# Moving the last gate quarter behind the last expert, and summing the outputs on VectorE

## The chip, the core and the metric

The kernel runs on one core of a Trainium2 chip. The metric is the time of one execution on the device in microseconds (us). A core has engines with a queue each: TensorE (PE in the profile: matrix products and transposes), VectorE (DVE), ScalarE (ACT), GpSimd (POOL) and the queue that issues most transfers (SP). An engine works through its queue in order and waits where an operand isn't ready. Matmul results go to PSUM (tiles pA, pB, pT, pG), all else lies in SBUF.

## The reference

A trunk of two layers over 512 tokens of width 1024. Layer 0 mixes with a state-space model and mean pools, layer 1 with stick-breaking attention. Each layer ends in a mixture of experts:

```
x = LN(alpha * x + mixer(x))
x = LN(alpha * x + MoE(x) + sigmoid(x Wg) * (p[i] Wp))

# attention, 16 heads of 64, strictly causal, by blocks of 128 queries
z = q k^T / 8
log_after = reverse cumsum of log_sigmoid(-z) over the causal keys, without the key itself
wts = exp(log_sigmoid(z) + log_after);  out = wts v

# LN: (x - mean) * rsqrt(var + 1e-5) * g + b
# MoE: 16 experts, router picks one group of four, in it the top two:
#   y_e = (silu(x W1) * (x W3)) W2,  MoE(x) = sum of gate * y_e over the token's two experts
```

All is float32; x is 512 x 1024, an expert's weights are 3 x 1024 x 512, Wg is 1024 x 1024 and Wp 256 x 1024.

## The kernel before

All matmuls that need float32 precision are done as three products of rounded parts: `split` (lines 84, 85) makes the high part with a ScalarE copy and the low part with a VectorE subtraction, `mm3` (89 to 91) issues the three. Weights come in pieces of 1 MB through a ring of 17 slots (tiles raw), each piece is split into w_0h, w_0l, w_2h, w_2l and so on. A scheduler orders the instructions of each engine by its own costs; the order is fixed when the program is built.

The tokens lie in four blocks of 128 rows: tiles x0r, listed `xt[0]` to `xt[3]`. `ffn` handles the experts in turn: each takes up to 96 tokens, gathered by index from a copy of x in memory (xd) with a transfer that POOL issues (line 936), turned, multiplied up (three 1024 x 512 pairs in all), through silu, multiplied down, and scattered to a table yd (line 942), two rows a token. Expert 12 is followed by a branch for tokens beyond the 96 (`overflow`). The last expert's output isn't scattered: it stays in SBUF as yl.

The gate sigmoid(x Wg) * (p Wp) is computed in four quarters of 256 columns (`gate`, lines 956 to 973). A quarter is 96 matmuls for x Wg (tile pG) and 24 for p Wp (tile pB), 128x256 each, in two halves of two blocks; then a sigmoid (966), a product (970) and, for each block, x = alpha * x + product (973). The tuple GATES sets where: quarter 0 ahead of the experts, quarters 1 to 3 behind experts 3, 6 and 10.

The tail (lines 1052 to 1076): the four tiles yt bring the two expert outputs of each token back, the last expert's product runs, and for each block and each half of 512 columns TensorE sums in PSUM: two matmuls with diagonal matrices of the token's gate values (dg) times yt (1068), and two with a one-hot matrix times yl (1071). VectorE adds x (1072) and takes statistics (1073); `ln_finish` (778 to 789) normalizes: bn_aggr and an addition (781, 782), the power -1/2 on POOL (783), and two steps over 1024 columns. The second is one VectorE step (789), or, with spread (blocks 0 to 2 of the tail), a ScalarE scaling (786) and a POOL addition (787). In layer 1 the block then goes out. In layer 0 it is turned (170) for the attention.

The attention (`attend`, 663 to 693) works on two heads at once, s = 0 and 1, and for each on four query blocks: scores (673 to 675), two sigmoids (678, 679), a scan (681), a product (682), then the weights are turned (686), copied (687) and multiplied with v (691). The two heads' products go to the lower and the upper half of one PSUM tile's partitions. Each is complete for one head before the other's, in the program's text.

The mixers' output projection (`out_proj`) adds x in `finish` (724), takes statistics (725) and calls `ln_finish` too.

## Time and profile before

| | us |
|---|---|
| median of three runs | 1267.3 (1264.76 to 1269.89) |
| the profiled execution | 1269.24 |
| its span in the trace | 1267.6 |
| TensorE busy | 1187.4 (94%) |
| VectorE busy | 972.6 (77%) |
| ScalarE busy | 748.4 (59%) |
| GpSimd busy | 152.2 (12%) |

The granted clock of TensorE over the span is 0.978. The stages as the trace has them: layer 0's mixer to about 210, its experts to 552, their tail to 587, the attention to 860, projection, normalization and router to 893, experts to 1236.6, tail to the end. Busy time is an average over these; a stage's limit is read from that stage.

### The profile page before, as it was taken

How to read it: one execution, taken by the hardware profiler on the slowest of the kernel's cores; microseconds unless marked ns; L12 is line 12 of the kernel's file. 1: busy time of each engine (PE TensorE's matmuls, PEld its weight loads, DVE VectorE, ACT ScalarE, POOL GpSimd, SP SyncE). 2: the span in 40 equal slices, each digit the busy share in tenths (PEclk: the TensorE clock that was granted, in tenths of full speed). 3: DMA queues.
4: the chain of work that ended last, by engine and by line, in shares of the span. 5: the costliest groups of instructions: out<-in, count | busy, mean ns of one | idle time of the engine just before them, and what ended most of it. 6: DMA issues, size and time to landing. Idle time of an engine off the chain costs nothing. (4 is left out here: it accounts for less than half of the span.)

```text
span 1267.6 us, 17418 instructions
## 1 busy us (share of the span) xinstructions
PE 1187.4 (94%) x6511; PEld 906.7 (72%) x6511; DVE 972.6 (77%) x1364; ACT 748.4 (59%) x1043; POOL 152.2 (12%) x160
## 2 busy tenths in 40 slices
PE   6958988999999999997999999998999999999895
PEld 5847778778787786756867877787677778787662
DVE  7996887896969967765477377868797887969676
ACT  4313523886868867842465455612687777868761
POOL 5010041010101000112000000012111000010004
PEclk9988999999999999998999999999999999999898
DMA  8235652998989998771113023543699797999842
GB/s 246 59 80 196 240 213 72 341 371 288 360 283 355 368 339 311 266 276 34 34 34 100 1 67 111 170 153 125 208 355 372 275 367 263 373 340 356 310 181 105
DMA packets 158165, 285.12 MB, mean 225 GB/s; under 512 B 19585, under 2 KB 43665, under 8 KB 157009
## 3 DMA queue, kind: packets, MB, share of 16 engines
q1 hardware_dynamic: 143760, 256.56, 58.0%
q0 software_dynamic: 9568, 25.19, 5.8%
q10 hardware_dynamic: 4736, 2.10, 0.6%
q8 instruction: 55, 0.90, 0.3%
q14 instruction: 46, 0.37, 0.1%
HBM read 272.02 MB, written 20.19 MB: 231 GB/s over the span
## 5 line engine op out<-in xcount | busy, mean ns | idle before, releaser
L85 DVE TENSOR_TENSOR w_0l<-raw,w_0h 128x1024 fp32r<-128x1024 f32 (+1 forms) x231 | 277.5, 1202 | 68.6 <-ACT w_0h L84 59.1
L84 ACT ACTIVATE w_0h<-raw 128x1024 fp32r<-128x1024 f32 (+1 forms) x233 | 242.8, 1042 | 76.8 <-PE pG L91 37.8
L85 DVE TENSOR_TENSOR w_2l<-raw,w_2h 128x1024 fp32r<-128x1024 f32 x205 | 249.7, 1218 | 21.9 <-ACT w_2h L84 21.7
L84 ACT ACTIVATE w_2h<-raw 128x1024 fp32r<-128x1024 f32 x205 | 216.6, 1056 | 44.6 <-PE pA L91 33.6
L89 PE MATMUL pA<-w_0h,g 128*96 128x512 f32 x256 | 105.6, 412 | 0.5 <-ACT g L84 0.5
L90 PE MATMUL pA<-w_0l,g 128*96 128x512 f32 x256 | 101.9, 398 | 0.0
L91 PE MATMUL pA<-w_2h,g 128*96 128x512 f32 x256 | 101.7, 397 | 0.0
L91 PE MATMUL pA<-w_0h,g 128*96 128x512 f32 x256 | 101.6, 397 | 0.0
L90 PE MATMUL pA<-w_2l,g 128*96 128x512 f32 x256 | 101.2, 395 | 0.0
L89 PE MATMUL pA<-w_2h,g 128*96 128x512 f32 x256 | 101.2, 395 | 0.0
L942 POOL DMA_INDIRECT yd<-ysb,ixm x30 | 32.1, 1071 | 489.5 <-ACT ysb L1038 489.5
L91 PEld LDWEIGHTS pA<-w_2h,g 128*96 128x96 f32 x256 | 41.6, 163 | 18.0
L91 PEld LDWEIGHTS pA<-w_0h,g 128*96 128x96 f32 x256 | 41.6, 163 | 17.9
L90 PEld LDWEIGHTS pA<-w_2l,g 128*96 128x96 f32 x256 | 41.6, 163 | 17.9
L89 PEld LDWEIGHTS pA<-w_2h,g 128*96 128x96 f32 x256 | 41.4, 162 | 17.8
L90 PEld LDWEIGHTS pA<-w_0l,g 128*96 128x96 f32 x256 | 42.2, 165 | 15.5 <-DVE w_0l L85 1.1
L89 PEld LDWEIGHTS pA<-w_0h,g 128*96 128x96 f32 x256 | 42.1, 164 | 14.9 <-ACT g L84 0.9
L936 POOL DMA_INDIRECT xg<-xd,ixm x32 | 35.3, 1104 | 138.1 <-PE pT L985 95.7
L89 PE MATMUL pB<-w_0h,sT 128*96 128x512 f32 x128 | 50.6, 396 | 1.2 <-ACT sT L84 1.2
L91 PE MATMUL pB<-w_0h,sT 128*96 128x512 f32 x128 | 51.2, 400 | 0.0
L90 PE MATMUL pB<-w_0l,sT 128*96 128x512 f32 x128 | 50.7, 396 | 0.4 <-DVE w_0l L85 0.4
L89 PE MATMUL pB<-w_2h,sT 128*96 128x512 f32 x128 | 51.0, 398 | 0.0
(439 smaller groups left out, 2874.2 us busy)
## 6 DMA issues: line engine op xcount, KB each, us to landing
raw<-in_moe_w_dram SPq DMA_DIRECT2D x192, 1024.0 KB, 11.4
raw<-in_sb_w_qkv_dram SPq DMA_DIRECT2D x12, 1024.0 KB, 7.9
raw<-in_ple_w_gate_dram SPq DMA_DIRECT2D x8, 1024.0 KB, 10.5
yt<-yd SPq DMA_DIRECT2D x8, 1024.0 KB, 8.0
raw<-in_ab_w_out_dram SPq DMA_DIRECT2D x4, 1024.0 KB, 6.4
xd<-x0r POOLq DMA_DIRECT2D x8, 512.0 KB, 2.9
raw<-in_sb_w_out_dram SPq DMA_DIRECT2D x4, 1024.0 KB, 6.0
raw<-in_ab_w_in_dram SPq DMA_DIRECT2D x3, 1024.0 KB, 9.7
```

The source lines that it names most:

```text
L84: return (self.nc.scalar.activation(hi, src, AF.Copy), (self.nc.gpsimd if pool else self.nc.vector).tensor_tensor(lo, src, hi.bitcast(F32) ...
L85: (self.nc.gpsimd if pool else self.nc.vector).tensor_tensor(lo, src, hi.bitcast(F32), op=OP.subtract))
L89: t.matmul(out, s[0], m[0], start=first, stop=False)
L90: t.matmul(out, s[0], m[1], start=False, stop=False)
L91: t.matmul(out, s[1], m[0], start=False, stop=last)
L936: return nc.gpsimd.indirect_dma_start(out=xgs[:CAP, e % 2, :], out_offset=None, in_=xd[:, :], in_offset=bass.IndirectOffsetOnAxis(ap=self. ...
L942: nc.gpsimd.indirect_dma_start(out=yd[:, :], out_offset=bass.IndirectOffsetOnAxis(ap=self.iy[:CAP, e:e + 1], axis=0), in_=src[:CAP], in_of ...
```

## The change

It has four parts. First, quarter 3 of the gate moves behind the last expert's down projection, and quarters 1 and 2 to experts 4 and 9; the scaling of x by alpha, for quarter 3's columns, becomes four steps of its own (line 1047 of the new file). Second, the tail's sum: instead of diagonal matrices on TensorE, VectorE adds each of the eight gate-weighted yt halves to x (line 1069, 128x1024 each); TensorE keeps the one-hot products. Third, statistics: bn_stats and bn_aggr go; the additions also give row sums (accum_out), ScalarE squares the centred block with a row sum, and no block is spread to POOL any more. Fourth, in the attention the two heads' products with v alternate, key block by key block, behind both heads' turns.

```diff
-GATES = (-1, 3, 6, 10)
+GATES = (-1, 4, 9, 15)
-SPF = (0, 1, 2)
-SPM = ()
# attend
+                kw = [self.half4("kw"), self.half4("kw")]
                 for s in range(2):
...
                     v.tensor_tensor(sg[:, :n - 1], sg[:, :n - 1], kp[:, 1:n], op=OP.mult)
+                for s in range(2):
+                    kp, sg = kw[s][:, :512], kw[s][:, 512:]
                     pT = self.bank("T", "pT")
                     for kb in range(qb + 1):
...
                     nc.any.tensor_copy(kp[:, :n], pT[:, :n])
-                    rows = slice(s * 64, s * 64 + 64)
-                    hc = (pg * 4 + h) * 64
-                    for kb in range(qb + 1):
-                        nc.tensor.matmul(po[rows, qs], vs[:, kb, hc:hc + 64], kp[:, kb * 128:(kb + 1) * 128],
-                                         start=(kb == 0), stop=(kb == qb))
+                for kb in range(qb + 1):
+                    for s in range(2):
+                        hc = (pg * 4 + 2 * o + s) * 64
+                        nc.tensor.matmul(po[s * 64:s * 64 + 64, qs], vs[:, kb, hc:hc + 64],
+                                         kw[s][:, kb * 128:(kb + 1) * 128], start=(kb == 0), stop=(kb == qb))
# out_proj, finish
-            v.scalar_tensor_tensor(xt[i][:, h], xt[i][:, h], ALPHA, ps, op0=OP.mult, op1=OP.add)
-            v.bn_stats(st[:, i, nh * 6:(nh + 1) * 6], xt[i][:, h])
+            v.scalar_tensor_tensor(xt[i][:, h], xt[i][:, h], ALPHA, ps, op0=OP.mult, op1=OP.add,
+                                   accum_out=st[:, i, nh:nh + 1])
# ln_finish
-        v.bn_aggr(mv[:, 0:2], st)
-        v.tensor_scalar(mv[:, 2:3], mv[:, 1:2], EPS, None, op0=OP.add)
+        v.tensor_scalar(mv[:, 0:1], st[:, 0:1], st[:, 1:2], -1.0 / D, op0=OP.add, op1=OP.mult)
+        sq = self.half4("sq")
+        nc.scalar.activation(sq, x, AF.Square, bias=mv[:, 0:1], accum_out=mv[:, 1:2])
+        v.tensor_scalar(mv[:, 2:3], mv[:, 1:2], 1.0 / D, EPS, op0=OP.mult, op1=OP.add)
         nc.gpsimd.tensor_tensor(mv[:, 3:4], mv[:, 2:3], self.mhalf, op=OP.pow)
-        v.scalar_tensor_tensor(x, x, mv[:, 0:1], self.lng, op0=OP.subtract, op1=OP.mult)
-        if spread:
-            nc.scalar.activation(x, x, AF.Copy, scale=mv[:, 3:4])
-            nc.gpsimd.tensor_tensor(x, x, self.lnb, op=OP.add)
-        else:
-            v.scalar_tensor_tensor(x, x, mv[:, 3:4], self.lnb, op0=OP.mult, op1=OP.add)
+        v.scalar_tensor_tensor(x, x, mv[:, 0:1], self.lng, op0=OP.add, op1=OP.mult)
+        v.scalar_tensor_tensor(x, x, mv[:, 3:4], self.lnb, op0=OP.mult, op1=OP.add)
# gate(c)
-                    v.scalar_tensor_tensor(x, x, ALPHA, sg[:, i], op0=OP.mult, op1=OP.add)
+                    if c < 3:
+                        v.scalar_tensor_tensor(x, x, ALPHA, sg[:, i], op0=OP.mult, op1=OP.add)
+                    else:
+                        v.tensor_tensor(x, x, sg[:, i], op=OP.add)
# behind expert 13
+                for i in range(NT):
+                    v.tensor_scalar(xt[i][:, 768:], xt[i][:, 768:], ALPHA, None, op0=OP.mult)
# tail
+        gate(3)
+        for i in range(NT):
+            for k in range(2):
+                v.scalar_tensor_tensor(xt[i], yts[i][:, k * D:(k + 1) * D], self.gates[:, k, i], xt[i],
+                                       op0=OP.mult, op1=OP.add)
         for i in range(NT):
             for nh in range(2):
...
-                for k in range(2):
-                    nc.tensor.matmul(p, dg[:, k * NT + i], yts[i][:, k * D + nh * 512:k * D + (nh + 1) * 512],
-                                     start=(k == 0), stop=False)
                 for a in range(2):
...
-                v.tensor_tensor(xt[i][:, h], p, xt[i][:, h], op=OP.add)
-                v.bn_stats(st[:, i, nh * 6:(nh + 1) * 6], xt[i][:, h])
-            self.ln_finish(xt[i], st[:, i], f"{layer}f{i}", i in SPF)
+                v.scalar_tensor_tensor(xt[i][:, h], p, 1.0, xt[i][:, h], op0=OP.mult, op1=OP.add,
+                                       accum_out=st[:, i, nh:nh + 1])
+            self.ln_finish(xt[i], st[:, i], f"{layer}f{i}")
```

The order of an engine's instructions is the scheduler's, so it is shown at three places. First TensorE in the first pair of heads of the attention. Before, around the products with v (691), the turns (686), scores (673 to 675) and the projection (89 to 91):

```order
L89 MATMUL pA<-x2Th_5581,w_4h 128x512
L691 MATMUL pA<-kw,v_5656 64x128
L686 MATMUL pT<-ident,kw 128x128 x2
L691 MATMUL pA<-kw,v_5656 64x128 x2
L686 MATMUL pT<-ident,kw 128x128 x3
L673 MATMUL pB<-KH,QS 128x512
L691 MATMUL pA<-kw,v_5656 64x128 x2
L674 MATMUL pB<-KL,QS 128x512
L675 LDWEIGHTS identb
```

After (the same lines are 691, 686 and 672 to 674, the projection 87 to 89):

```order
L691 MATMUL pA<-kw,v_5640 64x128 x4
L686 MATMUL pT<-ident,kw 128x128 x3
L89 MATMUL pA<-x2Th_5564,w_0l 128x512
L686 MATMUL pT<-ident,kw 128x128 x4
L87 MATMUL pA<-x2Th_5565,w_4h 128x512
L691 MATMUL pA<-kw,v_5640 64x128 x6
L686 MATMUL pT<-ident,kw 128x128 x4
L88 MATMUL pA<-x2Tl_5567,w_4h 128x512
L89 MATMUL pA<-x2Th_5565,w_4l 128x512
```

A group of products held one head's key blocks; now a group of four or more holds those of both heads in turn, behind the turns of both.

The second place is VectorE at the tail of layer 1. Before, from the last expert's output on (x0r_1245 holds blocks 0 and 1, x0r_1248 blocks 2 and 3):

```order
L1060 SCALAR_TENSOR_TENSOR yl_11783<-pB,gs,yl_11783 96x512 x2
L1072 TENSOR_TENSOR x0r_1245<-pA,x0r_1245 128x512
L1073 BN_STATS st1f<-x0r_1245 128x6
L1072 TENSOR_TENSOR x0r_1245<-pA,x0r_1245 128x512
L1073 BN_STATS st1f<-x0r_1245 128x6
L781 BN_AGGR mv1f_11856<-st1f 128x2
L782 TENSOR_SCALAR mv1f_11856<-mv1f_11856 128x1
L784 SCALAR_TENSOR_TENSOR x0r_1245<-x0r_1245,mv1f_11856,ln_ffn_11562 128x1024
L1072 TENSOR_TENSOR x0r_1245<-pA,x0r_1245 128x512
```

After, from the same instruction on (968 is the gate's product, 974 its addition, 1069 the sums of the expert outputs, 1077 the addition of the one-hot product):

```order
L1063 SCALAR_TENSOR_TENSOR yl_11614<-pB,gs,yl_11614 96x512 x2
L968 TENSOR_TENSOR sg<-sg,pB 128x512
L974 TENSOR_TENSOR x0r_1245<-x0r_1245,sg 128x256 x2
L1069 SCALAR_TENSOR_TENSOR x0r_1245<-yt_0_11606,gates_8027,x0r_1245 128x1024
L1069 SCALAR_TENSOR_TENSOR x0r_1245<-yt_1_11608,gates_8027,x0r_1245 128x1024
L1069 SCALAR_TENSOR_TENSOR x0r_1245<-yt_0_11606,gates_8027,x0r_1245 128x1024
L1069 SCALAR_TENSOR_TENSOR x0r_1245<-yt_1_11608,gates_8027,x0r_1245 128x1024
L968 TENSOR_TENSOR sg<-sg,pB 128x512
L1077 SCALAR_TENSOR_TENSOR x0r_1245,st1f<-pA,x0r_1245 128x512
L974 TENSOR_TENSOR x0r_1248<-x0r_1248,sg 128x256 x2
L1069 SCALAR_TENSOR_TENSOR x0r_1248<-yt_2_11610,gates_8027,x0r_1248 128x1024
```

The sums of blocks 0 and 1 stand ahead of the second half of the gate, those of blocks 2 and 3 behind it, and the normalization, which followed each block, comes behind all eight.

The third place is VectorE at layer 1's router, before the change (85 splits the turned x, 803 takes the logits):

```order
L85 TENSOR_TENSOR ol_5909<-pT,oh_5908 128x4x128
L85 TENSOR_TENSOR ol_6858<-pT,oh_6857 128x4x128
L85 TENSOR_TENSOR ol_5909<-pT,oh_5908 128x4x128
L85 TENSOR_TENSOR ol_6858<-pT,oh_6857 128x4x128
L803 COPY rt<-pB 32x512
L825 TENSOR_TENSOR rt<-rt,rbias 128x64
L828 TENSOR_TENSOR rt<-rt 128x32
```

After:

```order
L83 TENSOR_TENSOR ol_5893<-pT,oh_5892 128x4x128
L83 TENSOR_TENSOR ol_6842<-pT,oh_6841 128x4x128
L1047 TENSOR_SCALAR x0r_1245<-x0r_1245 128x256 x2
L1047 TENSOR_SCALAR x0r_1248<-x0r_1248 128x256 x2
L801 COPY rt<-pB 32x512
L823 TENSOR_TENSOR rt<-rt,rbias 128x64
L826 TENSOR_TENSOR rt<-rt 128x32
```

The four scalings of quarter 3's columns (1047) stand right ahead of the logits' copy (now 801). They write x, which the copies to xd read.

## Rows read from the trace of the kernel before

**Rows 1.** By stretch: us, busy PE, PEld, DVE, ACT, POOL; clock, DMA share, GB/s.

```profile
587.00:860.00 273.00, 269.57 (x1434) 207.98 (x1434) 171.30 (x277) 127.91 (x267) 10.88 (x9) 1.00 0.24 80
...
893.00:1236.60 343.60, 334.42 (x1738) 249.57 (x1738) 275.39 (x292) 261.25 (x318) 34.23 (x33) 0.99 0.89 314
1236.60:1267.60 31.00, 17.50 (x49) 8.77 (x47) 21.27 (x30) 4.13 (x4) 12.98 (x7) 0.82 0.24 98
```

**Rows 2.** POOL's timeline: start, length, line, tiles, the idle time before.

```profile
1109.40 1.09 POOL L942 DMA_INDIRECT yd<-ysb,ixm  x1 [15.30 <-ACT ysb L1038]
1127.07 0.94 POOL L942 DMA_INDIRECT yd<-ysb,ixm  x1 [14.90 <-ACT ysb L1038]
```

**Rows 3.** The table by stretch, an expert without a gate and one with it.

```profile
1032.00:1049.70 17.70, 17.70 (x118) 15.11 (x117) 11.32 (x13) 10.82 (x14) 0.94 (x1) 1.00 1.03 376
1127.07:1159.16 32.09, 32.09 (x207) 26.89 (x206) 21.90 (x26) 21.73 (x27) 1.90 (x2) 1.00 0.97 344
```

**Rows 4.** TensorE's timeline at the start of layer 1's tail.

```profile
1236.47 1.88 PE L1068 MATMUL pA<-yt,dg 128*128 128x512 f32 x4
```

**Rows 5.** VectorE's timeline in quarter 3 of layer 1's gate.

```profile
1133.46 0.69 DVE L970 TENSOR_TENSOR sg<-sg,pB 128x512 f32<-128x512 f32 x1 [4.46 <-PE pB L91]
...
1134.72 0.75 DVE L973 SCALAR_TENSOR_TENSOR x0r<-x0r,sg 128x256 f32<-128x256 f32 x2
```

**Rows 6.** VectorE's timeline in layer 1's tail.

```profile
1242.74 0.15 DVE L782 TENSOR_SCALAR mv1f<-mv1f 128x1 f32<-128x1 f32 x1
1242.81 1.27 DVE L784 SCALAR_TENSOR_TENSOR x0r<-x0r,mv1f,ln_ffn 128x1024 f32<-128x1024 f32 x1
1244.01 0.68 DVE L1072 TENSOR_TENSOR x0r<-pA,x0r 128x512 f32<-128x512 f32 x1
...
1247.17 2.05 DVE L784 SCALAR_TENSOR_TENSOR x0r<-x0r,mv1f,ln_ffn 128x1024 f32<-128x1024 f32 x1
...
1259.85 1.28 DVE L789 SCALAR_TENSOR_TENSOR x0r<-x0r,mv1f,ln_ffn 128x1024 f32<-128x1024 f32 x1 [0.44 <-POOL mv1f L783]
```

**Rows 7.** ScalarE's and POOL's timelines in layer 1's tail.

```profile
1244.55 1.15 ACT L786 ACTIVATE x0r<-x0r,mv1f 128x1024 f32<-128x1024 f32 x1 [7.19 <-POOL mv1f L783]
...
1245.78 2.35 POOL L787 TENSOR_TENSOR x0r<-x0r,ln_ffn 128x1024 f32<-128x1024 f32 x1 [1.27 <-ACT x0r L786]
...
1258.29 1.53 POOL L783 TENSOR_TENSOR mv1f<-mv1f,mhalf 128x1 f32<-128x1 f32 x1
```

**Rows 8.** TensorE's and VectorE's timelines in layer 0's tail.

```profile
552.28 7.03 PE L1068 MATMUL pA<-yt,dg 128*128 128x512 f32 x16
...
581.37 1.27 DVE L789 SCALAR_TENSOR_TENSOR x0r<-x0r,mv0f,ln_ffn 128x1024 f32<-128x1024 f32 x1
...
590.85 0.39 PE L90 MATMUL pA<-w_2l,x2Th 128*128 128x512 f32 x1
```

**Rows 9.** TensorE's timeline in the attention: one head alone.

```profile
752.59 0.43 PE L691 MATMUL pA<-kw,v 128*64 128x128 f32 x2
752.95 0.49 PE L674 MATMUL pB<-KL,QS 128*128 128x512 f32 x1
753.37 0.65 PE L691 MATMUL pA<-kw,v 128*64 128x128 f32 x4
753.95 0.77 PE L686 MATMUL pT<-ident,kw 128*128 128x128 f32 x5
```

**Rows 10.** The same, two heads' products side by side.

```profile
662.40 0.67 PE L691 MATMUL pA<-kw,v 128*64 128x128 f32 x8
662.99 0.44 PE L686 MATMUL pT<-ident,kw 128*128 128x128 f32 x2
```

**Rows 11.** DMA issues (median to landing), then POOL's and VectorE's timelines at layer 1's router.

```profile
xd<-x0r POOLq DMA_DIRECT2D x8, 512.0 KB, 2.9
...
872.27 0.59 POOL L928 DMA_DIRECT2D xd<-x0r  x1 [1.66 <-DVE x0r L789]
...
876.12 0.68 DVE L803 COPY rt<-pB 32x512 f32<-32x512 f32 x1 [1.15 <-PE pB L797]
```

More of the change, by code (lines that the diff above doesn't have):

```diff
@@ L682, in attend @@
                     v.tensor_tensor(sg[:, :n - 1], sg[:, :n - 1], kp[:, 1:n], op=OP.mult)
+                for s in range(2):
+                    kp, sg = kw[s][:, :512], kw[s][:, 512:]
                     pT = self.bank("T", "pT")
@@ L738, in out_proj @@
                 self.ln_setup("ln_mix", layer)
-                st = self.cp.tile([128, NT, 12], F32, tag="st", bufs=2, name=f"st{layer}m")
+                st = self.cp.tile([128, NT, 2], F32, tag="st", bufs=2, name=f"st{layer}m")
                 self.load_p(layer)
@@ L751, in out_proj @@
             finish(1, i, p)
-            self.ln_finish(xt[i], st[:, i], f"{layer}m{i}", i in SPM)
+            self.ln_finish(xt[i], st[:, i], f"{layer}m{i}")
     def load_p(self, layer):
@@ L776, in ln_setup, with ln_finish @@
         self.lng, self.lnb = t[:, 0, :], t[:, 1, :]
-    def ln_finish(self, x, st, name, spread=False):
+    def ln_finish(self, x, st, name):
         nc, v = self.nc, self.nc.vector
         mv = self.cp.tile([128, 4], F32, tag="mv", bufs=4, name="mv" + name)
-        v.bn_aggr(mv[:, 0:2], st)
-        v.tensor_scalar(mv[:, 2:3], mv[:, 1:2], EPS, None, op0=OP.add)
+        v.tensor_scalar(mv[:, 0:1], st[:, 0:1], st[:, 1:2], -1.0 / D, op0=OP.add, op1=OP.mult)
+        sq = self.half4("sq")
+        nc.scalar.activation(sq, x, AF.Square, bias=mv[:, 0:1], accum_out=mv[:, 1:2])
+        v.tensor_scalar(mv[:, 2:3], mv[:, 1:2], 1.0 / D, EPS, op0=OP.mult, op1=OP.add)
         nc.gpsimd.tensor_tensor(mv[:, 3:4], mv[:, 2:3], self.mhalf, op=OP.pow)
-        v.scalar_tensor_tensor(x, x, mv[:, 0:1], self.lng, op0=OP.subtract, op1=OP.mult)
-        if spread:
-            nc.scalar.activation(x, x, AF.Copy, scale=mv[:, 3:4])
-            nc.gpsimd.tensor_tensor(x, x, self.lnb, op=OP.add)
-        else:
-            v.scalar_tensor_tensor(x, x, mv[:, 3:4], self.lnb, op0=OP.mult, op1=OP.add)
+        v.scalar_tensor_tensor(x, x, mv[:, 0:1], self.lng, op0=OP.add, op1=OP.mult)
+        v.scalar_tensor_tensor(x, x, mv[:, 3:4], self.lnb, op0=OP.mult, op1=OP.add)
     def logits(self, X, pr, i):
@@ L961, in gate @@
             for b in range(2):
-                p = self.bank("A" if c < ng else "B", "pG").rearrange("p (i n) -> p i n", i=2)
+                p = self.bank("A" if c < ng or c == 3 else "B", "pG").rearrange("p (i n) -> p i n", i=2)
                 for i in range(2):
@@ L1042, in ffn @@
             if e == NE - 3:
-                oht, dg = self.last_onehot()
+                oht = self.last_onehot()
                 self.ln_setup("ln_ffn", layer)
+                for i in range(NT):
+                    v.tensor_scalar(xt[i][:, 768:], xt[i][:, 768:], ALPHA, None, op0=OP.mult)
             if e in GATES:
@@ L1061, in ffn @@
                                    op0=OP.mult, op1=OP.subtract)
-        st = self.cp.tile([128, NT, 12], F32, tag="st", bufs=2, name=f"st{layer}f")
+        gate(3)
+        st = self.cp.tile([128, NT, 2], F32, tag="st", bufs=2, name=f"st{layer}f")
+        for i in range(NT):
+            for k in range(2):
+                v.scalar_tensor_tensor(xt[i], yts[i][:, k * D:(k + 1) * D], self.gates[:, k, i], xt[i],
+                                       op0=OP.mult, op1=OP.add)
         for i in range(NT):
@@ L1066, in ffn @@
                 p = self.bank("A", "pA")
-                for k in range(2):
-                    nc.tensor.matmul(p, dg[:, k * NT + i], yts[i][:, k * D + nh * 512:k * D + (nh + 1) * 512],
-                                     start=(k == 0), stop=False)
                 for a in range(2):
-                    nc.tensor.matmul(p, oht[:CAP, i * 128:(i + 1) * 128], yl[:CAP, a, h], start=False, stop=(a == 1))
-                v.tensor_tensor(xt[i][:, h], p, xt[i][:, h], op=OP.add)
-                v.bn_stats(st[:, i, nh * 6:(nh + 1) * 6], xt[i][:, h])
-            self.ln_finish(xt[i], st[:, i], f"{layer}f{i}", i in SPF)
+                    nc.tensor.matmul(p, oht[:CAP, i * 128:(i + 1) * 128], yl[:CAP, a, h], start=(a == 0), stop=(a == 1))
+                v.scalar_tensor_tensor(xt[i][:, h], p, 1.0, xt[i][:, h], op0=OP.mult, op1=OP.add,
+                                       accum_out=st[:, i, nh:nh + 1])
+            self.ln_finish(xt[i], st[:, i], f"{layer}f{i}")
             if last:
@@ L1095, in last_onehot @@
         nc.scalar.activation(gs, pg[:, 0:1], AF.Copy)
-        dg = self.half4("dg").rearrange("p (x t) -> p x t", x=8)
-        for x in range(2 * NT):
-            nc.scalar.activation(dg[:, x], self.ident, AF.Copy, scale=self.gates[:, x // NT, x % NT])
-        return oht, dg
+        return oht
     def overflow(self, layer, xd, yd):
```

2 lines of the change are left out of this document (removed).

## The prediction

> **What bounds the kernel now.** I read the table by stretch first [rows 1]. In the attention stretch (587 to 860) TensorE is busy 269.57 of 273 us and VectorE 171.30, so what shortens TensorE's work there shortens the kernel. In the second run of experts TensorE is busy 334.42 of 343.60 us, the DMA share is 0.89: TensorE first, the transfers close behind. In the last 31 us TensorE is busy 17.50, VectorE 21.27, and the granted clock is 0.82: a chain, not a full engine. Then I read the rows that give each part a price.
>
> **The gate quarter that leaves the experts.** Scatters follow each other by 17.67 us where no gate stands between (1109.40 to 1127.07) [rows 2], and by 32.09 where quarter 3 does (from 1127.07 on: the second window of [rows 3] is that distance). The gate costs 32.09 − 17.67 = 14.42 us, all of it TensorE. Each layer's experts get shorter by that, if the weights keep up. Two windows on the same expert pace show the DMA share: 1.03 in one without a gate, 0.97 in that with the gate [rows 3]. Without a gate the queues are full. The gates stood behind experts 3, 6 and 10; now behind 4 and 9, so runs of 4, 3, 4 and 5 experts become 5, 5 and 6. The last run holds the overflow branch, in which few weights are used. I charge +1 us for both layers, between 0 and +5 (an expert's six pieces of 1.05 MB at the 344 GB/s of the gate's window [rows 3] take 18.3, 0.6 more than 17.67, over eight experts).
>
> **The tail of layer 1.** T0 is where the first L1068 matmul stands, 1236.47; the span ends at 1267.6, so 31.1 us [rows 4]. Now gate(3) begins at T0, and its two halves end at 7.2 and 14.4. VectorE has, in its order: the first half's product, 0.69, and its two additions, 0.33 apart after the row of two with 0.75 [rows 5], from 7.6 to 9.05; then four sums over 128x1024. These have the form of L784 and L789 (two f32 sources in SBUF, one scalar per partition): 1.27 and 1.28, the next instruction 1.20 after the start [rows 6]. Four make 4.8, to 13.85. The second product waits for its matmuls until 14.8. From there: product, one 512-column addition with row sum, two additions and four sums, 0.7 + 0.7 + 0.75 + 4.8 = 7.0, to 21.8. Then seven additions of 0.7 (4.9), eight 1024-column steps (9.6) and eight small ones of 0.15 (1.2) are left, 15.7 in all; the last tile adds hops through ScalarE (squares, priced by L786 at 1.15 [rows 7]) and POOL (pow 1.53 [rows 7]). Up to block 2 the other blocks' work covers these; behind the last addition nothing is left to cover them: 0.15, square 1.15, 0.15, pow 1.53 and the last step 1.28, 4.3 in a row, with some 0.3 for each of two hops. Walking through the order so, the last normalizing step ends at 39.7; the same step ends at 1259.85 + 1.28 = 1261.13 before, 6.5 ahead of the end, so the new end is T0 + 46.2. That is 15.1 longer, against 14.42 saved: **+0.7**. The POOL addition, beside which L784 took 2.05 instead of 1.27 [rows 6, 7], is gone, and that is counted. Row sums out of an addition show in no row of before: I charge 0.07 for each read of the sum, by which a one-column step holds up the next (1242.74 to 1242.81 [rows 6]); the bounds are 0 and 0.25, which is 0 to 2 over a tail's eight. Range −1 to +3.
>
> [...]
>
> **The tail of layer 0.** Here the next consumer is the value projection of the attention, which needs the turned x of all four blocks. T0 is again the first L1068 row, 552.28. The last normalizing step starts at 581.37 and ends at 582.64, and the matmul at 590.85 is one behind which the projection has TensorE to itself: T0 + 38.6, and 8.2 behind the normalizing step [rows 8]. After the change the walk above holds for this layer too; a split of projection weights (1.2) has moved into the wait of the last block and overfills it, so the last step ends near T0 + 40.5. Behind it stand the same turned blocks and weight splits as before; VectorE's own work there is about 6 us (four splits of 0.7, two of 1.2, a hop), the rest was waiting for turned blocks. So the same point comes between 46.5 and 48.7; I take 47.2. It is 8.6 later, less the gate's 14.42: **−5.8**, between −9 (if the projection fills more of the wait) and −1 (if TensorE, idle for longer than in the tail that now has a clock of 0.82 [rows 1], runs the first projection matmuls at the low level). It gains more than layer 1, since before the change the turns and splits of the next stage stood in the same chain, and now they lie in its waits.
>
> **The heads of a pair.** The product of weights and values is 160 matmuls of 64 columns (two records each). One alone holds TensorE 0.36 us (752.59 to 752.95), two of one head 0.58 (753.37 to 753.95) [rows 9], so each further one costs 0.22. Where the first two of each head happen to stand side by side, the four take 0.59 (662.40 to 662.99) [rows 10]: as long as two. By the timeline and these prices the 53 groups of before sum to 39.7 us. In the new order 52 groups remain, but with the heads in turn. Priced by the rows (a lone one or two of different heads 0.36, three or four 0.58, five or six 0.80, seven 1.02), 23 × 0.36 + 5 × 0.36 + 4 × 0.58 + 4 × 0.59 + 5 × 0.80 + 3 × 0.81 + 8 × 1.02 = 29.4. TensorE gets 10.3 us. Since the second head's turn and copy now precede both products, some waits come in; I take **−8.3**, bounds −10.4 and −2.
>
> **The mixers' normalization.** bn_stats and bn_aggr leave VectorE, a Square on ScalarE and two hops come into the same chain: I take 0 with −2 to +2. One wait is added: four scalings of 128x256 stand in VectorE's queue ahead of the router's first copy, and wait until the copies of x to memory, which read the same rows, have landed. The last of these was issued at 872.27 and lands after 2.9, at 875.2; the router's copy started at 876.12 [rows 11]. So 0.9 us are left, less the last scaling. Behind it on VectorE stand the router and the first gather.
>
> **Sum.** 1.0 + 0.7 − 5.8 − 8.3 + 0 = −12.4. The profiled execution took 1269.24 us, 1.9 above the median of 1267.3. Taken off both, 1256.8 and 1254.9; I say 1256.
>
> **Rivals.**
> 1. *The tail costs more than the gate saves.* Eight sums in an in-order VectorE stand behind the first half of the gate. If one takes 2.4 instead of 1.20, half of them hide no longer: (9.6 − 1.0 of slack) × 2 = +17.2, which gives 1273, slower. It decides from 2.1 us a sum, where (8 × 0.9 − 1.0) × 2 = 12.4. Against it: the 1.20 of L784 [rows 6]. Chance 0.06. [...]
> 2. *The alternation saves nothing.* The halves run at the same time only when both are ready; the group that began at 662.40 was one. If the order's waits eat the gain (VectorE and ScalarE set the pace), −8.3 becomes −1, and the time 1263. For it: VectorE busy 171 of 273 with long scans; against: TensorE's 269.57. Chance 0.16.
> 3. *The weights fall behind* in runs of five and six: each expert is then paced by the transfers, +5, so 1260. For it: shares of 1.03; against: the overflow branch and two gates let the lead recover. Chance 0.10.
> 4. *The scalings hold up the router* by 2 us a layer: 1260. Chance 0.06.
> The forecast itself has 0.62.
>
> **How the numbers follow.** The bounds sum to −22 and +7 if all fall on one side; as they hardly do, 1247 to 1267 holds 8 in 10. About 0.5%, 6.3 us, can be told from no change: faster is below 1261. The forecast gives 0.56 of faster, rival 2 gives 0.05, rivals 3 and 4 0.08; slower takes rival 1 and little else, 0.08; the same gets the rest, 0.23, so faster 0.69.
>
> **What would show it.** Right: quarter 3's matmuls behind the last down projection at pitch 0.12; new sums at 1.27; the tail of layer 1 at 46 us from T0; L691 groups of 29 us in sum, attention near 265 us; scatters at 17.67 in runs of five. Wrong: sums over 2 us; idle of TensorE in the attention above 8 us; ScalarE waiting for a DMA in expert 8, 9, 14 or 15; the router's copy waiting for the scalings.

## The result, and the profile after

The changed kernel takes 1254.51 us (median of 4, 1252.52 to 1256.82) against 1268.60 before (four runs: the three given above and one of 1272.34): a ratio of 0.989, 95% interval 0.9854 to 0.9925. The profiled execution took 1252.52 with a span of 1250.9, that is 16.7 less than the profiled one of before; the medians differ by 14.1, so the account below is 2.6 us more generous than the runs. All steps and rows are read from one profiled execution of each kernel.

The time is right. The parts are not all where the forecast put them. Here is the span cut at marks that both traces have, with the forecast's term beside each step:

| step | before | after | change | forecast |
|---|---|---|---|---|
| layer 0: last normalizing step to the router's copy | 4.14 | 7.62 | +3.5 | 0 |
| router's copy to expert 0's scatter | 45.24 | 46.25 | +1.0 | 0 |
| scatters of experts 0 to 12 | 255.32 | 240.88 | −14.4 | −14.4 |
| over the branch: scatter 12 to 13 | 22.40 | 19.43 | −3.0 | 0 |
| scatter 14 to the projection's 26th matmul in the trace | 53.14 | 57.48 | +4.3 | +8.6 |
| first to last product with v | 190.63 | 183.10 | −7.5 | −8.3 |
| to the mixer's last normalizing step | 46.85 | 47.99 | +1.1 | 0 |
| layer 1: to the router's copy | 4.14 | 7.67 | +3.5 | 0 |
| router's copy to expert 0's scatter | 45.40 | 46.41 | +1.0 | 0 |
| scatters of experts 0 to 12 | 255.32 | 240.90 | −14.4 | −14.4 |
| over the branch | 25.51 | 20.54 | −5.0 | 0 |
| scatter 14 to the end | 44.12 | 57.89 | +13.8 | +15.1 |

The steps left out change by 0.6 together. The same table by stretch, for the attention, the second experts and the last tail (columns as in [rows 1]):

```profile
578.00:844.00 266.00, 261.00 (x1439) 197.68 (x1438) 167.21 (x278) 130.82 (x274) 10.00 (x9) 1.00 0.26 86
882.00:1206.00 324.00, 317.58 (x1621) 233.62 (x1620) 272.06 (x287) 255.64 (x306) 36.97 (x32) 1.00 0.93 333
1206.00:1250.90 44.90, 19.78 (x137) 17.88 (x135) 28.70 (x48) 8.13 (x12) 5.83 (x4) 0.70 0.17 70
```

TensorE is as full as before in the first two. The tail, 31 us in [rows 1], is 45, and the granted clock in it is 0.70 instead of 0.82. An expert late in a run of five, and the next with the gate, answer to [rows 2, 3]:

```profile
1066.13:1083.81 17.68, 17.68 (x85) 12.69 (x84) 15.81 (x17) 14.65 (x19) 2.46 (x2) 1.00 1.03 378
1083.81:1115.88 32.07, 32.07 (x207) 26.90 (x206) 21.93 (x26) 21.72 (x27) 1.90 (x2) 1.00 0.77 278
```

The pace held at 17.68 with the DMA share at 1.03: the weights kept up. VectorE's timeline in layer 1's tail answers to [rows 5, 6]; the gate starts on TensorE at 1206.01, so that is T0:

```profile
1213.47 0.69 DVE L968 TENSOR_TENSOR sg<-sg,pB 128x512 f32<-128x512 f32 x1 [5.79 <-PE pB L89]
1214.19 0.76 DVE L974 TENSOR_TENSOR x0r<-x0r,sg 128x256 f32<-128x256 f32 x2
1214.87 4.87 DVE L1069 SCALAR_TENSOR_TENSOR x0r<-yt,gates,x0r 128x1024 f32<-128x1024 f32 x4
1220.67 0.69 DVE L968 TENSOR_TENSOR sg<-sg,pB 128x512 f32<-128x512 f32 x1 [0.93 <-PE pB L89]
...
1227.95 0.08 DVE L1077 DVE_READ_ACCUMULATOR x0r<-pA,x0r 128x1 f32 x1
...
1241.38 0.15 DVE L784 TENSOR_SCALAR mv1f<-mv1f 128x1 f32<-128x1 f32 x1 [1.37 <-ACT sq L783]
1241.44 1.28 DVE L786 SCALAR_TENSOR_TENSOR x0r<-x0r,mv1f,ln_ffn 128x1024 f32<-128x1024 f32 x1
1243.16 1.28 DVE L787 SCALAR_TENSOR_TENSOR x0r<-x0r,mv1f,ln_ffn 128x1024 f32<-128x1024 f32 x1 [0.44 <-POOL mv1f L785]
```

Four sums take 4.87, 1.2 each: the price read from L784. All sixteen of both layers are 1.27 to 1.28 long, as L784 alone was. The first product comes 7.5 behind T0 (forecast 7.6), the second 14.7 (14.8), the last step ends at T0 + 38.4 (39.7). Reading a row sum is a row of its own, 0.08 long, and the next instruction starts where it starts: next to nothing. In layer 0 the corresponding rows [rows 8] are:

```profile
575.62 1.27 DVE L787 SCALAR_TENSOR_TENSOR x0r<-x0r,mv0f,ln_ffn 128x1024 f32<-128x1024 f32 x1
...
581.91 0.39 PE L87 MATMUL pA<-w_2h,x2Th 128*128 128x512 f32 x1
```

From T0 (537.41) the last step ends after 39.5, and the projection has TensorE to itself 44.5 after T0 (forecast 47.2). This last row is the projection's 26th recorded matmul, as 590.85 is in [rows 8]. TensorE's timeline in the attention, against [rows 9, 10]:

```profile
629.48 0.66 PE L691 MATMUL pA<-kw,v 128*64 128x128 f32 x8
630.62 0.52 PE L686 MATMUL pT<-ident,kw 128*128 128x128 f32 x3 [0.48 <-DVE kw L680]
...
634.65 1.09 PE L691 MATMUL pA<-kw,v 128*64 128x128 f32 x14
635.66 0.50 PE L89 MATMUL pA<-x2Th,w_4l 128*128 128x512 f32 x1
```

Each of these 160 matmuls leaves two records, 320 in all. Seven matmuls of two heads take 1.01 (634.65 to 635.66), where four of one head took 1.02 in the kernel before:

```profile
643.76 1.09 PE L691 MATMUL pA<-kw,v 128*64 128x128 f32 x8
644.78 0.55 PE L686 MATMUL pT<-ident,kw 128*128 128x128 f32 x3
```

Behind the first group TensorE waits 0.48 for the other data. Summed, the 52 groups take 31.9 us, 29.4 by the prices. The router's rows [rows 11] show what was held up:

```profile
859.55 0.69 DVE L1047 TENSOR_SCALAR x0r<-x0r 128x256 f32<-128x256 f32 x3
863.71 0.29 DVE L1047 TENSOR_SCALAR x0r<-x0r 128x256 f32<-128x256 f32 x1 [3.47 <-DMA xd<-x0r]
863.92 0.67 DVE L801 COPY rt<-pB 32x512 f32<-32x512 f32 x1
```

VectorE stands 3.47 us in front of the fourth scaling, waiting for xd to land, and the router's copy stands behind it. The landing itself is longer than it was. The issues around the last copy of layer 1 (KB each, us from issue to landing), between 871 and 874 us of the kernel before:

```profile
xd<-x0r POOLq DMA_DIRECT2D x1, 512.0 KB, 4.5
```

and between 856 and 858 us of the changed one:

```profile
raw<-in_moe_w_dram SPq DMA_DIRECT2D x1, 1024.0 KB, 6.1
xd<-x0r POOLq DMA_DIRECT2D x1, 512.0 KB, 7.1
```

SP's load of a megabyte of weights now goes out within half a microsecond of the copy, where it went out 5.2 us ahead of it (867.09 for a copy at 872.27), and the copy takes 7.1 instead of 4.5.

### The profile page after: what moved, and what is told of

Same layout as the page of the kernel before. It is cut to its first block, busy times and chain, and to the rows that moved or that the text cites. A ratio compares the mean times of both kernels' runs of the same rounds, so it can differ in the third digit from the quotient of the medians.

```text
span 1250.9 us, 17354 instructions
## 1 busy us (share of the span) xinstructions
PE 1157.1 (93%) x6447; PEld 889.3 (71%) x6447; DVE 971.1 (78%) x1393; ACT 752.4 (60%) x1051; POOL 144.7 (12%) x154
## 5 line engine op out<-in xcount | busy, mean ns | idle before, releaser
L940 POOL DMA_INDIRECT yd<-ysb,ixm x30 | 37.4, 1247 | 473.5 <-ACT ysb L1039 455.2
L88 PEld LDWEIGHTS pA<-w_0l,g 128*96 128x96 f32 x256 | 41.8, 163 | 14.8 <-DVE w_0l L83 1.1
L679 DVE TENSOR_TENSOR_SCAN kw<-kw 128x128 f32<-128x128 f32 (+3 forms) x64 | 50.2, 812 | 0.9 <-ACT kw L676 0.6
```

The source lines that it names most:

```text
L88: t.matmul(out, s[0], m[1], start=False, stop=False)
L679: v.tensor_tensor_scan(rv, rv, rv, 1.0, op0=OP.mult, op1=OP.min)
L940: nc.gpsimd.indirect_dma_start(out=yd[:, :], out_offset=bass.IndirectOffsetOnAxis(ap=self.iy[:CAP, e:e + 1], axis=0), in_=src[:CAP], in_of ...
```

## The experiments

Ratios are to the kernel before, with 95% intervals. Each batch of runs had its own runs of the kernel before, whose medians lie between 1267.6 and 1270.4, so kernels of different batches compare by their ratios. Steps are those of the table above.

### The scalings in the router

```diff
-                for i in range(NT):
-                    v.tensor_scalar(xt[i][:, 768:], xt[i][:, 768:], ALPHA, None, op0=OP.mult)
...
+                    v.scalar_tensor_tensor(x, x, ALPHA, sg[:, i], op0=OP.mult, op1=OP.add)
```

> The changed kernel with one edit: quarter 3's scaling by alpha goes back into the gate's addition, so the four scalings that stand ahead of the router's copy of the logits are gone. Theory: each router starts its copy 3.5 us earlier (about 4.1 us behind the last normalizing step, as before the change, instead of 7.6), and nothing else was waiting, so two layers give 6 to 7.5 us: about 1247.5, ratio to the kernel before near 0.983. Rival: the router's chain or the first gather ends on the transfers of xd anyway, since the gather reads xd; then the copy starts earlier but the first gather moves by less than 1 us and the time stays near 1254.

Measured: 1248.54, ratio 0.9831 (0.9812 to 0.9849), 6 us under the change by the medians, 7.5 by the ratios. In layer 1 the step to the router's copy is 3.82, in layer 0 5.31 (there the copy waits for TensorE's logits); the scatter of expert 0 moves with it. So the scalings' wait cost 2 to 4 us a layer, and some 1 us more up to the first scatter. The copy still lands after 7.2 us in layer 0, but no cheap instruction waits for it in front of the router.

### The order of the tail

The sums stand ahead of the gate, the scaling is tied behind expert 13's product:

```diff
+            self.mul = v.tensor_tensor(sg, sg, hh[1][:CAP], op=OP.mult)
...
+                with self.tc.issue_after(self.mul.ins):
                     for i in range(NT):
                         v.tensor_scalar(xt[i][:, 768:], xt[i][:, 768:], ALPHA, None, op0=OP.mult)
...
+        for i in range(NT):
+            for k in range(2):
+                v.scalar_tensor_tensor(xt[i], yts[i][:, k * D:(k + 1) * D], self.gates[:, k, i], xt[i],
+                                       op0=OP.mult, op1=OP.add)
         gate(3)
```

> The changed kernel with the order of the tail turned: VectorE's eight sums of the expert outputs stand ahead of the last gate quarter in the program, and the scaling by alpha is pinned behind expert 13's product, so that neither it nor its wait stands in the router. Theory: the sums run while TensorE does the gate, so behind the second half of the gate only a product, additions and the normalization are left: the last normalizing step comes at T0 + 33 instead of 38.4 in both layers, 5 us each, and the router gives 7 as in the kernel with the scaling in the gate: about 1237, ratio near 0.976. Rival: the expert outputs land too late; then VectorE's queue stands behind its first sum, the splits of the gate's weights come late, TensorE waits in front of the gate, and the tail gains nothing: about 1247.

Measured: 1234.56, ratio 0.9727 (0.9709 to 0.9745). VectorE in layer 1's tail, sums (1068) and last steps:

```profile
1189.50 1.28 DVE L1068 SCALAR_TENSOR_TENSOR x0r<-yt,gates,x0r 128x1024 f32<-128x1024 f32 x1
...
1205.87 0.69 DVE L968 TENSOR_TENSOR sg<-sg,pB 128x512 f32<-128x512 f32 x1 [3.29 <-PE pB L89]
...
1223.58 1.28 DVE L787 SCALAR_TENSOR_TENSOR x0r<-x0r,mv1f,ln_ffn 128x1024 f32<-128x1024 f32 x1 [0.44 <-POOL mv1f L785]
```

All sums are done before the second product, for which VectorE now waits 3.29 us. From that product to the end of the last step it is 19.0 us, in the changed kernel 23.8. The last normalizing steps end at T0 + 33.4 and T0 + 33.7, as forecast. Scatter 14 to the end falls from 57.89 to 54.38, the same step of layer 0 by 8.6; both routers are at 3.8.

Then, on top of that, the tail of blocks 0 and 1 goes between the halves of the gate; `rest(b)` holds the one-hot products and the normalization of two blocks:

```diff
                 for i in range(2):
                     x = xt[2 * b + i][:, cs]
...
+                if rest:
+                    rest(b)
...
+        def rest(b):
+            for i in (2 * b, 2 * b + 1):
...
-        gate(3)
+        gate(3, rest)
```

> The kernel with the sums first, and one edit more: the tail of blocks 0 and 1 (one-hot products, additions, normalization) is written behind the first half of the last gate quarter, that of blocks 2 and 3 behind the second. Theory: behind the second half only two blocks are left, 19.0 us from the gate's last matmul to VectorE's last step become 12 to 13.5, while the gate itself ends about 1.9 us later, since the first blocks' one-hot products go ahead of the second half: 4 us a layer in both, so about 1226.5 against 1234.6, ratio to the kernel before near 0.966. Rival: the normalization's hops through ScalarE and POOL, not VectorE's work, set the end; then two blocks in a row take as long as the last two of four, the gate's 1.9 us come on top, and the time is 1234 to 1238.

Measured: 1233.08, ratio 0.9712 (0.9687 to 0.9736): not told apart from the version before it. Layer 1's tail did as the theory says, 54.38 to 49.05, with 9.7 us from the second product (1214.27) to the end of VectorE's last step. Layer 0's tail became 0.8 longer, its router took 5.35 instead of 3.79, and the step over layer 1's branch took 23.69 instead of 20.82, at a granted clock of 0.86 instead of 1.00 behind a branch row as long as before (3.58 and 3.62). The forecast of 4 us in each layer held in one.

### Who sums

The changed kernel with the diagonal products on TensorE again:

```diff
-                v.scalar_tensor_tensor(xt[i], yts[i][:, k * D:(k + 1) * D], self.gates[:, k, i], xt[i],
-                                       op0=OP.mult, op1=OP.add)
+                    nc.tensor.matmul(p, dg[:, k * NT + i], yts[i][:, k * D + nh * 512:k * D + (nh + 1) * 512],
+                                     start=(k == 0), stop=False)
```

> The changed kernel with its second part undone: TensorE sums the expert outputs with diagonal matrices again, behind the moved gate, and VectorE adds the result with a row sum. Theory: the tail then hangs on TensorE, gate 14.4 and eight times 2.19 (1.72 for the diagonal products, 0.47 for the one-hot), to T0 + 31.9, and the last block's normalization, 5 us behind it, ends near T0 + 37, against 38.4 in the changed kernel: layer 1 is the same within 2 us, layer 0 the same within 3. So summing on VectorE paid nothing where it was put, behind the first half of the gate. Rival: the sums on VectorE are what made the moved gate affordable; then this kernel is slower than the changed one by 6 us or more.

Measured: 1253.71, ratio 0.9875 (0.9851 to 0.9898). Layer 1's tail is 60.14 (57.89 with the sums on VectorE), layer 0's 56.39 (57.48), the rest equal. The last normalizing steps end at T0 + 39.2 and T0 + 39.4, some 2 us behind what was expected. Where they were put, the sums on VectorE earned nothing.

### The alternating heads

Alone, in the kernel before:

```diff
-                    for kb in range(qb + 1):
-                        nc.tensor.matmul(po[rows, qs], vs[:, kb, hc:hc + 64], kp[:, kb * 128:(kb + 1) * 128],
...
+                for kb in range(qb + 1):
+                    for s in range(2):
...
+                        nc.tensor.matmul(po[s * 64:s * 64 + 64, qs], vs[:, kb, hc:hc + 64],
```

> The kernel before with one part of the change: the two heads' products with v alternate. Theory: the two halves of TensorE's columns work side by side whenever both heads' weights are ready, and TensorE is the bound there, so the stretch from the first to the last L691 row falls from 190.6 us to about 183 and the whole time by 7 to 8.5 us, a ratio near 0.994. Rival: the shorter attention seen in the changed kernel comes from the moved gate (other weights in flight, another clock); then this kernel stays within 2 us of the one before.

Measured: 1264.65, ratio 0.9964 (0.9948 to 0.9980), 5.7 us by the medians, less than the 7 to 8.5 expected. The products' stretch is 183.45, so the 7.2 us are the alternation's. The step behind it gives 1.0 back, and layer 1's router 2.1. The last is the clock: the stretch that ends with the router's copy in this kernel, then in the kernel before,

```profile
862.00:872.44 10.44, 8.49 (x81) 8.11 (x82) 7.41 (x12) 2.39 (x4) 2.05 (x2) 0.67 0.55 200
```

```profile
866.00:876.12 10.12, 6.07 (x81) 5.80 (x82) 8.97 (x14) 2.28 (x4) 2.05 (x2) 1.00 0.73 273
```

The same 81 matmuls are busy 8.49 us at a granted clock of 0.67, against 6.07 at 1.00. The alternation doesn't always bring this: with the third part beside it (below) the same step takes 3.83. The other way round, the changed kernel with the lines above undone:

> The changed kernel with its fourth part undone: one head's products with v are complete before the other's. Theory: the stretch from the first to the last L691 row goes back from 183.1 to about 190.6 us, and 1 us of it is given back in the projection behind, so the kernel is 6 to 7.5 us slower than the changed one, near 1261. Rival: next to the moved gate the alternation is worth only what its run alone gave, 4.5 us (1259), because some 2 us return in the router.

Measured: 1261.77, ratio 0.9939 (0.9918 to 0.9961); stretch 190.31. Inside the change the alternation is worth 7 us by the medians; 7.2 in the stretch, less 1.0 that the step behind it gives back.

### The statistics

The third part alone in the kernel before:

```diff
-            v.bn_stats(st[:, i, nh * 6:(nh + 1) * 6], xt[i][:, h])
+                                   accum_out=st[:, i, nh:nh + 1])
...
-        v.bn_aggr(mv[:, 0:2], st)
...
+        nc.scalar.activation(sq, x, AF.Square, bias=mv[:, 0:1], accum_out=mv[:, 1:2])
...
-        if spread:
-            nc.scalar.activation(x, x, AF.Copy, scale=mv[:, 3:4])
-            nc.gpsimd.tensor_tensor(x, x, self.lnb, op=OP.add)
```

> The kernel before with the third part of the change alone: row sums from the additions, squares on ScalarE, no block spread to POOL; the gate, TensorE's sums and the heads' order as before. Theory: in the mixers nothing moves (within 0.5 us a layer up to the router's copy); in the tail VectorE's 5.1 us a block fall below TensorE's 2 x 2.19, so TensorE sets the pace, and the last normalizing step of layer 1 ends near T0 + 23.3 instead of 24.7. In all 1 to 4 us less, ratio 0.997 to 0.999. Rival: the hops through ScalarE in the chain cost more than bn_stats did, 0.5 us a block: 2 to 4 us more.

Measured: 1261.20, ratio 0.9924 (0.9900 to 0.9947), over twice the most that was expected, and not where it was expected. The mixers and layer 1's tail move by less than 1.3 us each (44.39 for 44.12 in the tail, whose last normalizing step ends at T0 + 24.9 and not at 23.3). Scatter 14 to the 26th projection matmul falls from 53.14 to 45.05. This kernel's stretch between the two, then that of the kernel before:

```profile
570.00:587.00 17.00, 13.87 (x73) 10.57 (x72) 15.82 (x26) 7.30 (x13) 2.71 (x2) 1.00 0.19 63
```

```profile
569.00:586.00 17.00, 10.16 (x39) 7.25 (x38) 15.86 (x20) 5.36 (x8) 9.73 (x6) 0.73 0.13 40
```

POOL is busy 2.71 instead of 9.73, since the additions of three blocks no longer run there; TensorE gets 73 matmuls through instead of 39, at a clock of 1.00 instead of 0.73. VectorE's normalizing steps tell how much of this is POOL's. In layer 0's tail, beside POOL's additions and then without them:

```profile
567.93 2.70 DVE L784 SCALAR_TENSOR_TENSOR x0r<-x0r,mv0f,ln_ffn 128x1024 f32<-128x1024 f32 x1
```

```profile
565.80 1.28 DVE L786 SCALAR_TENSOR_TENSOR x0r<-x0r,mv0f,ln_ffn 128x1024 f32<-128x1024 f32 x1
```

Three such steps took 2.70, 2.66 and 2.34; without POOL's additions they take 1.28, 1.28 and 1.27: 3.9 us. From T0 to the end of the last normalizing step the tail is 4.4 shorter. The other 3.7 us lie behind that step, where the clock went from 0.72 to 1.00, and are not surely this part's: the kernel with the longer lead (below) has the old tail and gets nearly as much there. The copy of x to memory is slow here too (7.3 us in layer 1, 4.5 with the alternating heads alone), so it is this part that brings SP's load forward: in every kernel that has it the load goes out 0.3 us ahead of the copy, in every other one 5.2.

Both parts together, that is the changed kernel with the gate and the sums as before:

```diff
-GATES = (-1, 4, 9, 15)
+GATES = (-1, 3, 6, 10)
...
-        gate(3)
```

> The kernel before with the third and the fourth part of the change (statistics, alternating heads), without the first two: the gate's last quarter stays behind expert 10 and TensorE keeps the sum. Theory: alone, the two parts gave 8.4 to 8.7 and 4.5 to 5.7 us; together about 13, so this kernel runs at about 1256.5, within 3 us of the whole change (1254.5), and the moved gate with its sums on VectorE earned next to nothing: what it saved in the experts it gave back in the tails and the routers. Rival: the parts overlap (both shorten what the same low clock had lengthened), together they give 8 to 9 us, 1261, and the moved gate has 6 us or more of the gain.

Measured: 1254.80, ratio 0.9895 (0.9870 to 0.9920), the whole change's 0.989 within the interval. By the traces (1250.6 and 1250.9), the moved gate with its sums adds to this kernel −28.8 in the experts, +14.0 and +13.5 in the tails, +7.4 around the routers and −5.1 over the branches. (With the gate goes a choice of PSUM tiles that the lines above don't show: quarter 3's products lie in those of pA. No run takes that apart.)

### The branch

Quarter 2 of the gate nearer to the branch, in the changed kernel:

```diff
-GATES = (-1, 4, 9, 15)
+GATES = (-1, 4, 10, 15)
```

> The changed kernel with quarter 2 of the gate behind expert 10 instead of 9, so that, as in the kernel before, two experts lie between it and the branch for tokens beyond the 96. Theory: the step over the branch (scatter of expert 12 to that of 13) is cheap in the changed kernel, 19.4 and 20.5 us, because the weight queues run dry while TensorE's queue crosses the branch; with the gate at 10 SP gets past the branch first and fills the queues, TensorE's branch row is 6.2 to 6.5 us again instead of 3.3, and the step takes 22.4 and 25.5 us: 6 to 8 us longer in all. Rival: the cheaper branch comes from what the change took out near it (the diagonal matrices on ScalarE); then the step stays at 19.4 and 20.5.

Measured: 1254.41, ratio 0.9883 (0.9862 to 0.9904); steps 19.42 and 20.48. The theory is out: at expert 10 the step is as at 9. The rival's reason is out too, by the run with TensorE's sums: it makes the diagonal matrices again, and its steps are 19.54 and 20.49. Then `(-1, 4, 11, 15)`:

> The changed kernel with quarter 2 of the gate behind expert 11, right ahead of the last expert before the branch. Theory, after the run with it behind expert 10: what counts is when SP's loads ahead of the branch have landed. With a gate right ahead they land early, SP passes the branch at least 2 us before TensorE, fills the queues, and the row of TensorE's branch is over 5.5 us instead of 3.3; the step over the branch is then 22 us or more in each layer. Rival: the step belongs to the new tail as a whole (fewer loads left to issue behind the branch), wherever the gate stands; then it stays at 19.4 and 20.5 and the branch row at 3.3 to 3.8.

One run gave 1258.47; steps 19.42 and 22.85, branch rows 3.56 and 3.90. SP's last wait at the branch ended 0.5 and 2.3 us behind TensorE's branch, and the rows stay short even with a gate beside the branch, so what the run was made to show did not happen. Layer 1's step is longer all the same, at a granted clock of 0.93. So I changed the loads themselves, fewer of them ahead in experts 11 and 12 of the changed kernel:

```diff
-            LA = 6 if e < 13 else 3
+            LA = 6 if e < 11 else 4 if e < 13 else 3
```

> The changed kernel with one edit: the weights' lookahead is 4 pieces instead of 6 in experts 11 and 12, so that two loads fewer stand in SP's queue ahead of the branch. Theory: SP passes the branch earlier than TensorE reaches it, sends its loads, and TensorE's branch row, 3.3 to 3.4 us in the changed kernel, becomes 5.5 us or more, as in the kernel before; the pause gets so long that the granted clock in the step falls below 0.95, and the step takes 22 to 25 us in both layers instead of 19.4 and 20.5, with 6 to 8 us on the whole. Rival: the branch row depends on the program, not on the loads; then row and step stay as they are in the changed kernel.

One run gave 1258.19; branch rows 4.48 and 5.12, steps 19.22 and 24.94. SP's last wait at the branch ends 3.8 and 2.0 us ahead of TensorE's branch, where it ended 1.6 and 1.4 behind it in the changed one. The rows grew as the theory says but by less, and only layer 1's step lengthened, with its clock at 0.86. One run each says little of the time; these two are read for their rows. The other way, more of them ahead in the kernel before:

```diff
-            LA = 6 if e < 13 else 3
+            LA = 6 if e < 11 else 8 if e < 13 else 3
```

> The kernel before with one edit: the lookahead is 8 pieces instead of 6 in experts 11 and 12, two loads more ahead of the branch. Theory: SP now waits for them at the branch until TensorE is across, TensorE's branch row falls from 6.2 and 6.5 us to about 3.4, the granted clock of the step rises to 1.00, and the step over the branch takes 19.4 to 20.6 us instead of 22.4 and 25.5: 6 to 8 us less, ratio near 0.9945. Rival: as for the kernel with the shorter lead, the row stays above 6 us, and the time with it.

Measured: 1261.84, ratio 0.9939 (0.9915 to 0.9962): two loads more ahead of the branch save 8 us by the medians. Layer 1's branch row and the steps over both branches, in the kernel before:

```profile
L1105 PEldq COMPARE_BRANCH  x1: 6532/6532/6532, 1176.5 to 1176.5; - x1
...
494.17:516.57 22.40, 19.54 (x92) 13.80 (x91) 17.25 (x24) 16.77 (x25) 1.10 (x2) 0.92 1.01 366
1176.84:1202.35 25.51, 20.86 (x92) 14.62 (x91) 17.00 (x24) 16.88 (x25) 1.09 (x1) 0.87 0.96 339
```

with the longer lead:

```profile
L1105 PEldq COMPARE_BRANCH  x1: 3792/3792/3792, 1169.4 to 1169.4; - x1
...
494.83:514.40 19.57, 18.52 (x92) 12.70 (x91) 17.00 (x24) 16.55 (x25) 1.10 (x2) 1.00 0.91 319
1169.79:1190.34 20.55, 18.43 (x92) 12.79 (x91) 16.90 (x24) 16.66 (x25) 1.09 (x1) 1.00 0.88 309
```

and in the changed kernel:

```profile
L1107 PEldq COMPARE_BRANCH  x1: 3319/3319/3319, 1150.9 to 1150.9; - x1
...
483.77:503.20 19.43, 18.37 (x91) 12.57 (x90) 16.87 (x24) 16.13 (x20) 1.10 (x1) 1.00 0.84 299
1151.23:1171.77 20.54, 18.04 (x91) 12.78 (x90) 16.78 (x24) 16.36 (x20) 1.09 (x1) 1.00 0.83 288
```

The row says min, median and longest in ns. In the kernel with the longer lead the short rows are the loads' doing, since the lead is all that was changed. The step holds a second thing, the granted clock: 1.00 here and in the changed kernel, where it was 0.92 and 0.87. A short row alone doesn't give that. Layer 1 of the changed kernel without the alternation:

```profile
L1105 PEldq COMPARE_BRANCH  x1: 3317/3317/3317, 1156.5 to 1156.5; - x1
...
1156.89:1180.42 23.53, 20.85 (x91) 14.66 (x90) 16.98 (x24) 16.46 (x20) 1.09 (x1) 0.85 0.76 255
```

The row is that of the changed kernel, the step 3.0 longer; with the scaling in the gate it is 23.66, at a clock of 0.86. And layer 0 of the kernel with parts three and four kept 1.00 behind a row of 6.77, with a step of 21.38. So some 3 of the 5.0 us of layer 1 belong to a clock that differs between traces, and what decides it is open. Open is also which line of the change put SP behind TensorE.

What TensorE's branch row waits for shows only in part. Under the row of the kernel before, the weight queue takes most of the transfers' time:

```profile
q1 hardware_dynamic: 1051, 2.09, 88.6%
...
q8 instruction: 1, 0.02, 1.0%
```

and under that of the changed one, nearly none:

```profile
q1 hardware_dynamic: 25, 0.05, 3.4%
...
q8 instruction: 1, 0.02, 1.8%
```

In both there is one packet in q8, a queue that the trace calls instruction. In all 28 branch rows this packet lands 1.3 to 1.5 us before the row ends (layer 1: 1.36 in the kernel before, 1.35 in the changed one). In the rows of 3.3 to 3.9 us it starts 0.9 to 1.6 us after the row (1.0 in the changed kernel), in the longer ones 2.0 to 5.0 (4.1 in the kernel before). What it carries, and that the row waits for it, the traces don't show. That it starts late because it waits behind the weights is argued, not shown.

The trace with the longer lead gains more than the two steps give: 11.8 us, of which they are 7.8 (it is the fastest of the six runs, 4.4 under their median). Layer 0's tail is 5.5 shorter in it (47.60 for 53.14), from the same lines of the program with some of TensorE's turns in another order; its clock is 1.00 in two places where it was 0.88 and 0.72 (table below). Why the clock stayed up there is open.

## Why the prediction came out right

- **Gate out of the experts, −14.4 a layer.** Right to a tenth of a us.
- **Weights fall behind, +1 (rival 3).** Didn't happen: 17.68 in the runs of five. That the DMA share was over 1 didn't mean that the lead was used up. (The first window of [rows 3] is not free of a gate, quarter 2 begins in it at 1041.97; windows from scatter to scatter have 1.01 to 1.05, so the reading stands.)
- **Tail of layer 1, +0.7.** It was −0.65 (13.77 − 14.42), by the steps that the prediction gave. Rival 1 is dead: no run shows a sum at its 2.4, they took 1.2 each.
- **Tail of layer 0, −5.8.** It was −10.1 (4.34 − 14.42), outside the term's own range of −9 to −1 (the low clock that its upper end supposed for the first projection matmuls didn't come: 1.00 behind the last step). Three stretches of this tail in four kernels, us and granted clock:

| | before | after | parts three and four | longer lead |
|---|---|---|---|---|
| scatter 14 to T0 | 14.57, 0.88 | 12.98, 1.00 | 13.01, 1.00 | 12.89, 1.00 |
| T0 to the end of the last normalizing step | 30.36, 0.91 | 39.48, 0.78 | 25.93, 1.00 | 29.78, 0.89 |
| from there to the 26th projection matmul | 8.21, 0.72 | 5.02, 1.00 | 4.56, 1.00 | 4.93, 1.00 |

  The forecast was 0, +10.1 and −1.5; measured are −1.6, +9.1 and −3.2. The step that failed is the reading of the old tail as a chain of fixed length. Ahead of T0 and behind the last step it held 5 us that the kernel with the longer lead, the same lines of the program at a granted clock of 1.00 there and some of TensorE's turns in another order, doesn't have; and VectorE's steps beside POOL's additions took 3.9 more than without them. Once both are gone, the moved gate costs the tail 14.0 (43.50 to 57.48), nearly all that it saves in the experts. So the reason given ("they lie in its waits") isn't borne out, though the sign was right.
- **Heads, −8.3.** The mechanism was right (seven products of two heads in 1.01 us, four of one head in 1.02), and rival 2 is out; −7.5 in the stretch, −6.4 with the 1.1 that came back behind it. The term missed that waits stand inside some groups (31.9 us of groups, not 29.4).
- **Router, 0, with rival 4 at 2 us a layer.** It was +4.5 a layer, and the sign that the prediction named for it, the router's copy waiting for the scalings, is in the rows. The margin of 0.9 us was worked out from a median landing of 2.9 over all eight copies of x. The last one of layer 1 took 4.5 in the kernel before and 7.1 in the changed one, since the third part brings a load of weights beside it. The rival's mechanism was right, its price less than half of the true one.
- **Branch.** −8.0, in no term and no rival; with layer 1's clock as in the kernel without the alternation it would be −5.

The two misses without a price in the sum, +9 in the routers and −8 at the branches, nearly cancel. That the sum of −12.4 lies so near the measured −14.1 is in part luck.

## What to carry to other kernels

Work that is moved off a full engine into a tail has to be paid there unless the tail's engine can do its own work at the same time. The quarter moved here earned nothing (ratio 0.989 against 0.9895 without it): what it saved in the experts went into the tails and the routers. Without the scalings in front of the router's copy it earned some 8 us (0.9831), and with VectorE's sums ahead of it 21 (0.9727). A median landing (2.9 us over the eight copies of x) isn't a bound for a wait that sits on the last of several transfers (4.5 and 7.1 for layer 1's last copy, before and after): read that transfer's own row, and look at what the change lets start beside it, and at what stands behind the waiting instruction in its queue. And look at the granted clock of a stretch before it gets a price: the same lines of the tail took 53.14 us in one trace and 47.60 in another, with the clock at 1.00 in two stretches where it had been 0.88 and 0.72.

## What the runs showed of the hardware

- In the kernel before, the changed one and those with quarter 2 behind expert 11 and with the shorter lead, a branch row of TensorE's queue took 3.3 to 3.9 us where SP's last wait at the branch ended behind TensorE's branch (layer 1 of the changed kernel: 1.4 us behind, row 3.32), and 4.5 to 6.5 where it ended ahead (layer 1 of the kernel before: 3.0 ahead, row 6.53). Two loads more in front of SP's branch turned 6.53 into 3.79. The packet of q8 landed 1.3 to 1.5 us before the end of each of the 28 rows.
- Over the step behind that row the granted clock was 1.00 in some kernels and 0.85 to 0.93 in others, behind long rows and short ones; in layer 1 of the kernel before (0.87) it was 0.50 from 1184.5 to 1191.3 us and 1.00 around that. Behind rows of 3.32 the step took 20.54 us at 1.00 (the changed kernel) and 23.53 at 0.85 (without the alternation); behind a row of 6.77 it took 21.38 at 1.00 (parts three and four), behind one of 6.23 22.40 at 0.92 (layer 0 of the kernel before).
- In the changed kernel a row sum out of a VectorE addition was a separate row of 0.08 us, out of a ScalarE Square one of 0.19.
- A VectorE step of 128x1024 with two operands in SBUF took 2.34 to 2.70 us beside a GpSimd addition of the same size in layer 0's tail, and 1.28 without it.
- The last copy of x of a layer (512 KB) took 2.9 and 4.5 us to land in the kernel before, where SP's last load had gone out 5.2 us ahead of it, and 7.0 and 7.1 in the changed one, where it went out 0.3 ahead.
